# Plain down chunks of a decoder trunk streamed as two products of 256 columns, with one order of terms

## The chip, the cores and the metric

The kernel runs on one core of a Trainium2 chip. The time is the device time of one execution in microseconds (us), and the number that counts is the median of several runs. The kernel before takes 1089.61 us, median of 3 runs from 1089.52 to 1090.16.

## The reference

One decoder layer over 256 tokens with 2048 features, all in float32: a normalised input goes through one projection to q, k, v and gates, two groups of eight attention heads follow, their outputs are projected back and added; then a squared-ReLU MLP with 8192 hidden features, and a last norm.

```python
h = rms_norm(x, norm1_g[l])
proj = h @ w_in[l]                      # 2048 -> 6152
...
x = x + mixed @ w_out[l]                # 2048 -> 2048
h = rms_norm(x, norm2_g[l])
x = x + jnp.square(jax.nn.relu(h @ w_mlp_in[l])) @ w_mlp_out[l]   # 2048 -> 8192 -> 2048
return rms_norm(x, final_norm_g)
```

The change lies in the last matrix product, with `w_mlp_out`: the down projection.

## The kernel before, in words

**Products in parts.** Each float32 operand is split into an upper part, which TensorE takes exactly (`hi`), and the rest (`lo`). A product of x and w is then three: x_hi w_hi, x_lo w_hi and x_hi w_lo, added up in PSUM. One operand stands in the array (an LDWEIGHTS of 128 x 128 ahead of each product), the other is streamed past it. A row of the profile such as `acc<-whi,big_lo` names the streamed operand first and the standing one second.

**Chunks and steps.** The weights are read in chunks of 512 columns. A chunk of the MLP has 16 tiles of 128 rows (`kt`), two of them to a step. For each step SyncE loads weights (`raw`, one megabyte for two steps), ScalarE writes the upper part (`whi`, L253) and VectorE the lower (`wlo`, L254), some steps ahead of the products, into a ring of tiles that the products give back.

**The MLP** goes in four rounds of 2048 hidden features. The chunks come in these forms:

- Up chunks ("u"): the weights stand, the activations `aT_hi`, `aT_lo` are streamed, 256 wide (`turned_product`, L417). Their results are squared and split into `big_hi`, `big_lo`, and a mixed form of them into `mix_hi`, `mix_lo`.
- Mixed down chunks (set `seven`): a form with seven block products instead of eight, which takes sums of weights and of activations. Here the activations stand and the weights are streamed, 256 wide, in the order hi hi, hi lo, lo hi (`seven_products`, L461). Each unit of four row tiles has four sub-steps: near, first, odd, even.
- Plain down chunks: the activations `big_hi`, `big_lo` stand, 128 tokens at a time, the weights are streamed 512 wide (`product`, L401). There are two in each round, and in the last round three.

The list `steps` (L138 to L159) sets the order by hand. A round opens with its four up chunks, among which the first down chunk of the round before is mixed in. Then comes a plain chunk by itself (8 steps), and after it four units of: near, first, odd of the second down chunk, a plain step of the third, even, another plain step. The last round opens with chunk 0 by itself and closes with chunk 3, the kernel's last. That one (`last_chunk`, L862) first does all 16 row tiles for the first 128 tokens, 512 wide, then twice for the second 128 tokens, 256 wide each, so that the end of the work on the first block lies beside products. Its first three steps of split weights go to the tiles of `aT_hi`, `aT_lo`, which are free by then.

**Order of the terms.** For the plain down chunks `product` takes the three terms in an order that `ORDERS` gives for each round: standing part and streamed part are hi hi, lo hi, hi lo in rounds 0 and 3; lo hi, hi hi, hi lo in round 1; hi lo, hi hi, lo hi in round 2. The last chunk uses hi hi, lo hi, hi lo. The attention's chunks that use `product` (v and o) have this order too.

**Places of the tiles.** All tiles that TensorE reads start at chosen offsets within 64 elements (constants L43 to L45). The split weights of plain down chunks and of the mixed steps both start at 8 (`NEAR`); `big_hi` and `big_lo` start at 32 and 48.

Of the kernel before, what the change touches and what calls it, by code (L numbers as in the profile page):

```python
# [28 lines left out]
CW = 512  # L29
# [13 lines left out]
LINE, NEAR, HIGH, LOW, GATED = 64, 8, 24, 56, 48  # L43
MIX_HI, MIX_LO = 24, 32
BIG_HI, BIG_LO = 32, 48  # L45
ORDERS = ((0, 1, 2), (1, 0, 2), (2, 0, 1), (0, 1, 2))
TURNED = "qku"
WARM, WARM2 = 8, 3

# [27 lines left out]
def kernel(  # L77
# [44 lines left out]
    for g, (vc, qc, kc, half, kind) in enumerate(groups):  # L122
        for what, c0 in (("q", qc), ("v", vc), ("k", kc)):
            cols = CW + NH if (g == 0 and what == "v") else CW
# [39 lines left out]
    raws, splits, spent = {}, {}, set()  # L164
# [62 lines left out]
    def split(i, j0=0, n=2):  # L227
        if i >= len(steps):
            return
        if j0:  # L230
            return split_rows(i, j0, n)
        ci, s, sub = steps[i]
        if sub:
            return split_seven(i)
        if ci == len(chunks) - 1 and s < 3:
            hi, lo = (a[:, 4 * s:4 * s + 4, :].rearrange("p (k j) s -> p k (j s)", k=2) for a in (aT_hi, aT_lo))
        else:
            what, cols = chunks[ci][0], chunks[ci][5]
            high, low = (HIGH, LOW) if what in TURNED else (NEAR, NEAR) if cols == CW else (GATED, HIGH - NEAR)
            hi, lo = (a.rearrange("p (j c) -> p j c", j=2) for a in part_tiles(i, 2 * cols, high, low))  # L240
        splits[i] = (hi, lo)
        split_rows(i, j0, n)
# [142 lines left out]
    accs = {}  # L385

    def operands(what, key):
        if what == "o":
            return yT_hi, yT_lo, key[0] * NH
        if what == "d":  # L390
            return *squares(), 0
        return aT_hi, aT_lo, 0

    def product(acc, a, kt, t, w, j, cols, go, end, order=(0, 1, 2)):

        (ah, al, base), (hi, lo) = a, w
        xh, xl = (p[:, base + kt, t * P:(t + 1) * P] for p in (ah, al))
        terms = ((xh, hi), (xl, hi), (xh, lo))
        for n, k in enumerate(order):
            x, part = terms[k]  # L400
            nc.tensor.matmul(acc, x, part[:, j, cols], start=go and n == 0, stop=end and n == 2,  # L401
                             skip_group_check=True)

    def turned_product(ci, i, j, kt, kts):


        if kt == 0:
            accs[ci] = [psum.tile([P, CW], F32, name="acc", bufs=4) for _ in range(2)]
        hi, lo = splits[i]
        terms = ((hi, aT_hi), (hi, aT_lo), (lo, aT_hi))  # L410
        order = [(b, n) for b in range(4) for n in range(3)]
        if i == j == 0:
            order.sort(key=lambda bn: bn[1])
        for b, n in order:
            acc = accs[ci][b // 2][:, b % 2 * SEQ:(b % 2 + 1) * SEQ]
            w, a = terms[n]
            nc.tensor.matmul(acc, w[:, j, b * P:(b + 1) * P], a[:, kt, :],  # L417
                             start=kt == 0 and b % 2 == 0 and n == 0, stop=kt == kts - 1 and n == 2,
                             skip_group_check=True)

    def products(i, j):
        ci, s, sub = steps[i]
        what, key, _, _, _, cols, kts = chunks[ci]
        if sub:
            return seven_products(i, j)
        kt = 2 * s + j
        if what in TURNED:
            return turned_product(ci, i, j, kt, kts)
        a = operands(what, key)
        if cols > CW:  # L430
            return gated_products(ci, i, j, kt, kts, a)
        if kt == 0:
            accs[ci] = [psum.tile([P, CW], F32, name="acc", bufs=4) for _ in range(TB)]
        go, end = kt == 0, kt == kts - 1
        order = ORDERS[key[0]] if what == "d" else (0, 1, 2)
        for t in range(TB):
            product(accs[ci][t], a, kt, t, splits[i], j, slice(0, CW), go, end, order)

    def seven_products(i, j):

        ci, s, sub = steps[i]
        if ci not in accs:
            accs[ci] = [psum.tile([P, CW], F32, name=n) for n in ("sc", "sc", "tr", "tr")]
        one_, two_, three, four = accs[ci]
        half, k1, k2 = CW // 2, 2 * s + j, 2 * s + 2 + j
        lower, upper = slice(0, P), slice(P, SEQ)
        h, m = squares(), (mix_hi, mix_lo)
        todo = {
            "near": ((one_, 0, h, k2, lower), (one_, half, m, k2, lower)),
            "first": ((three, 0, h, k1, lower),),  # L450
            "odd": ((two_, half, m, k2, upper), (four, 0, m, k1, upper)),
            "even": ((three, half, m, k1, lower), (two_, 0, h, k2, upper)),
        }[sub]
        begin = j == 0 and s == 0
        hi, lo = splits[i]
        for n, (bank, c0, (ah, al), k, tokens) in enumerate(todo):
            acc = bank[:, c0:c0 + half]
            fresh = begin and (bank, sub) in ((one_, "near"), (three, "first"), (two_, "odd"), (four, "odd")) and (
                bank is not one_ or n == 0)
            for x, (a, w) in enumerate(((ah, hi), (ah, lo), (al, hi))):  # L460
                nc.tensor.matmul(acc, a[:, k, tokens], w[:, j, n * half:(n + 1) * half], start=fresh and x == 0,  # L461
                                 stop=s == KT // 2 - 2 and j == 1 and x == 2, skip_group_check=True)

    def gated_products(ci, i, j, kt, kts, a):

        if kt == 0:
            accs[ci] = [psum.tile([P, 512], F32, name=n, bufs=k) for n, k in (("acc", 4), ("acc", 4), ("sc", 2))]
        half = CW // 2
        for t in range(TB):
            for acc, c0, c1, go in ((accs[ci][0][:, t * half:(t + 1) * half], 0, half, t == 0),  # L470
                                    (accs[ci][1 + t][:, :half + NH], half, CW + NH, True)):
                product(acc, a, kt, t, splits[i], j, slice(c0, c1), go and kt == 0, kt == kts - 1)
# [261 lines left out]
    def squares():  # L734
        return rows_at(big_hi, BIG_HI), rows_at(big_lo, BIG_LO)
# [86 lines left out]
    def add_down(acc, t, cs, n):  # L822

        nc.vector.scalar_tensor_tensor(
            xs[:, t, cs], acc[:, :cs.stop - cs.start], rstd2sq[:, t:t + 1], xs[:, t, cs], op0=ALU.mult, op1=ALU.add
        )
        if n is not None:
            if cs.stop < D_MODEL:
                square_and_gain(t, cs, n)
            else:  # L830
                unused = two.tile([P, CW], F32, name="nat")
                unused, xc, total = unused[:, :cs.stop - cs.start], xs[:, t, cs], ssq3[:, t, n:n + 1]
                nc.vector.tensor_tensor_reduce(unused, xc, xc, 1.0, 0.0, ALU.mult, ALU.add, total)
# [4 lines left out]
    def sum_before(t, n):  # L838
        s = ssq3s[:, t:t + 1]
        nc.vector.tensor_reduce(s, ssq3[:, t, :n], axis=mybir.AxisListType.X, op=ALU.add)  # L840
        nc.vector.tensor_scalar(s, s, D_MODEL * EPS, None, op0=ALU.add)
# [20 lines left out]
    def last_chunk(done):  # L862

        ci = len(chunks) - 1
        what, key, _, _, _, _, kts = chunks[ci]
        i0 = len(steps) - kts // 2
        c0 = D_MODEL - CW
        for t, a, b, n in ((0, 0, CW, 3), (1, 0, CW // 2, 3), (1, CW // 2, CW, 4)):
            acc = psum.tile([P, CW], F32, name="acc", bufs=4)
            for kt in range(kts):  # L870
                if t == 0 and kt % 2 == 0:
                    split(done + 1 + kt // 2)
                product(acc[:, :b - a], operands(what, key), kt, t, splits[i0 + kt // 2], kt % 2, slice(a, b),
                        kt == 0, kt == kts - 1)
                if t == 0:
                    run_side(2 * i0 + kt)
            if b == CW:
                sum_before(t, n)
            add_down(acc, t, slice(c0 + a, c0 + b), n)
            if b == CW:  # L880
                finish(t, n, slice(c0 + a, c0 + b))


    def run_side(n):
        for f, a in side.get(n, []):
            f(*a)

    for ci, (what, key, *_rest) in enumerate(chunks[:-1]):
# [9 lines left out]
        elif what in "qk":  # L898
# [3 lines left out]
            if what == "k":  # L902
                kind = groups[key][4]
                for h in range(4):
                    n = e + 6 + 7 * (h // 2)
# [63 lines left out]
    for i in range(final):  # L969
# [30 lines left out]
        for j in range(2):  # L1000
            products(i, j)
            run_side(2 * i + j)
    last_chunk(done)


# [28 lines left out]
```

## Time and profile before

| | |
|---|---|
| median of the runs | 1089.61 us (1089.52 to 1090.16) |
| the profiled execution | 1087.94 us |
| its span, first to last instruction | 1086.2 us |
| granted TensorE clock, mean | 0.997 |
| TensorE: busy, products | 1073.9 us, 7877 |
| weight loads: busy, loads | 1007.0 us, 7877 |
| VectorE, ScalarE, GpSimd busy | 800.3, 604.4, 28.0 us |
| read from memory | 205.93 MB |

PE is the product side of TensorE and PEld its weight loads, which go on beside the products; DVE is VectorE, ACT ScalarE, POOL GpSimd, SP SyncE. The profile gives for each group of instructions a busy time and a mean duration, but products overlap in the array: the next starts before the one ahead has ended. The chain of waits follows the work that ended last back to the beginning, and shows unbroken stretches of one line with their start, their length and the number of instructions. The windows give the busy time of each engine between two times, with the number of instructions. The attention ends and the MLP begins at 393.6 us.

### The profile page before, as it was taken

The numbers are of one execution on the slowest core, as the hardware profiler recorded it, in microseconds if no ns is written. First come the engines' busy times: TensorE is split into PE (matmuls) and PEld (weight loads), VectorE is DVE, ScalarE is ACT, GpSimd is POOL, SyncE is SP. The second block draws the span as 40 slices with busy tenths as digits, with TensorE's granted clock in tenths as the row PEclk, the third lists the DMA queues.
The fourth block names the chain that finished last, engine by engine and source line by source line (L and its number), as shares of the span: only waits on it lengthen the run. The fifth ranks groups of instructions, "written<-read, shape, count | busy, mean of one in ns | idle before, by whom it ended". The sixth has DMA issues, their size and how long they took to land.

```text
span 1086.2 us, 18976 instructions
## 1 busy us (share of the span) xinstructions
PE 1073.9 (99%) x7877; PEld 1007.0 (93%) x7877; DVE 800.3 (74%) x1076; ACT 604.4 (56%) x821; POOL 28.0 (3%) x42
## 2 busy tenths in 40 slices
PE   8999999999999999999999999999999999999996
PEld 7999899998988899998999998899998999999886
DVE  6667756667577666568877788887778886778885
ACT  6555545545454555565546665556665545666561
POOL 0010200000001000000000000000000000000000
PEclk9999999999999999999999999999999999999998
DMA  9764564655545566655675655665656665656552
GB/s 322 237 228 161 157 199 149 194 165 181 199 155 185 164 184 210 193 190 192 203 215 193 203 197 171 208 203 174 204 204 210 187 195 187 195 195 232 193 195 78
DMA packets 105394, 209.26 MB, mean 193 GB/s; under 512 B 3971, under 2 KB 5084, under 8 KB 105180
## 3 DMA queue, kind: packets, MB, share of 16 engines
q1 hardware_dynamic: 104412, 206.59, 58.3%
q8 instruction: 61, 1.00, 0.4%
q0 software_dynamic: 304, 1.06, 0.3%
q10 hardware_dynamic: 592, 0.40, 0.2%
q14 instruction: 25, 0.20, 0.1%
HBM read 205.93 MB, written 2.11 MB: 192 GB/s over the span
## 4 chain that ended last, share of the span: by engine, by line
PE 99%; DMA 0%; DVE 0%; POOL 0%; ACTq 0%; DVEq 0%; issue 0%
PE acc L417 48%; PE acc L401 34%; PE sc L461 7%; PE tr L461 5%; PE tr L350 1%; PE sc L691 1%; PE sc L401 1%; PE sc L647 1%; PE tr L675 0%; DMA xs<-in_x_dram 0%; PE sc L643 0%; PE sc L693 0%; PE sc L637 0%; PE sc L641 0%; DVE xs L859 0%; PE sc L695 0%
## 5 line engine op out<-in xcount | busy, mean ns | idle before, releaser
L254 DVE TENSOR_TENSOR wlo<-raw,whi 128x1024 fp32r<-128x1024 f32 (+2 forms) x327 | 394.0, 1220 | 155.2 <-ACT whi L253 152.9
L253 ACT ACTIVATE whi<-raw 128x1024 fp32r<-128x1024 f32 (+2 forms) x328 | 339.3, 1050 | 223.5 <-PE acc L417 130.4
L417 PE MATMUL acc<-aT_hi,whi 128*128 128x256 f32 x1536 | 425.6, 277 | 0.0
L417 PE MATMUL acc<-aT_hi,wlo 128*128 128x256 f32 x1536 | 424.0, 276 | 0.0
L417 PE MATMUL acc<-aT_lo,whi 128*128 128x256 f32 x1536 | 423.8, 276 | 0.0
L417 PEld LDWEIGHTS acc<-aT_hi,whi 128*128 128x128 f32 x1536 | 288.2, 188 | 1.2 <-issue 0.9
L417 PEld LDWEIGHTS acc<-aT_lo,whi 128*128 128x128 f32 x1536 | 288.2, 188 | 0.3
L417 PEld LDWEIGHTS acc<-aT_hi,wlo 128*128 128x128 f32 x1536 | 288.1, 188 | 0.1
L401 PE MATMUL acc<-whi,big_lo 128*128 128x512 f32 (+1 forms) x414 | 160.8, 388 | 0.0
L401 PE MATMUL acc<-whi,big_hi 128*128 128x512 f32 (+1 forms) x414 | 160.3, 387 | 0.0
L401 PE MATMUL acc<-wlo,big_hi 128*128 128x512 f32 (+1 forms) x414 | 160.0, 386 | 0.0
L401 PEld LDWEIGHTS acc<-wlo,big_hi 128*128 128x128 f32 x414 | 77.8, 188 | 15.9
L401 PEld LDWEIGHTS acc<-whi,big_lo 128*128 128x128 f32 x414 | 77.7, 188 | 15.2
L401 PEld LDWEIGHTS acc<-whi,big_hi 128*128 128x128 f32 x414 | 77.7, 188 | 15.2
L219 ACT ACTIVATE whi<-both 128x1024 fp32r<-128x1024 f32 x56 | 59.7, 1067 | 52.6 <-DVE both L224 24.8
L220 DVE TENSOR_TENSOR wlo<-both,whi 128x1024 fp32r<-128x1024 f32 x56 | 68.3, 1220 | 7.5 <-ACT whi L219 6.5
L337 DVE TENSOR_TENSOR big_lo<-nat,big_hi 128x512 fp32r<-128x512 f32 x32 | 22.2, 693 | 43.7 <-ACT big_hi L336 43.7
L401 PE MATMUL acc<-whi,aT_hi 128*128 128x512 f32 (+1 forms) x144 | 51.7, 359 | 0.0
L401 PE MATMUL acc<-whi,aT_lo 128*128 128x512 f32 (+1 forms) x144 | 51.0, 354 | 0.0
L401 PE MATMUL acc<-wlo,aT_hi 128*128 128x512 f32 (+1 forms) x144 | 51.0, 354 | 0.0
L219 ACT ACTIVATE whi<-raw 128x1024 fp32r<-128x1024 f32 x28 | 29.6, 1058 | 11.8 <-PE acc L401 6.4
L336 ACT ACTIVATE mix_hi<-nat 128x512 fp32r<-128x512 f32 x32 | 18.5, 625 | 29.9 <-DVE nat L761 29.9
(212 smaller groups left out, 1351.2 us busy)
## 6 DMA issues: line engine op xcount, KB each, us to landing
raw<-in_w_mlp_in_dram SPq DMA_DIRECT2D x64, 1024.0 KB, 5.7
raw<-in_w_mlp_out_dram SPq DMA_DIRECT2D x64, 1024.0 KB, 5.1
raw<-in_w_in_dram SPq DMA_DIRECT2D x42, 1024.0 KB, 5.1
raw<-in_w_out_dram SPq DMA_DIRECT2D x16, 1024.0 KB, 5.0
raw<-in_w_in_dram SPq DMA_DIRECT2D x4, 1040.0 KB, 8.5
xs<-in_x_dram SPq DMA_DIRECT2D x3, 512.0 KB, 9.7
raw<-in_w_in_dram SPq DMA_DIRECT2D x2, 512.0 KB, 5.4
big_lo<-rel_d POOLq DMA_DIRECT2D x1, 1024.0 KB, 7.2
```

Of the source, the lines that this page charges most:

```text
L219: nc.scalar.activation(hi, src, AF.Copy)
L220: nc.vector.tensor_tensor(lo, src, hi.bitcast(F32), op=ALU.subtract)
L253: nc.scalar.activation(hi[:, :, c:c + step], t[:, :, c:c + step], AF.Copy)
L254: nc.vector.tensor_tensor(lo, t, hi.bitcast(F32), op=ALU.subtract)
L336: nc.scalar.activation(hi, src, AF.Copy)
L337: nc.vector.tensor_tensor(lo, src, hi.bitcast(F32), op=ALU.subtract)
L350: nc.tensor.transpose(p[:, j * SEQ + t * P:j * SEQ + (t + 1) * P], xs[:, t, c:c + P], ident)
L401: nc.tensor.matmul(acc, x, part[:, j, cols], start=go and n == 0, stop=end and n == 2, skip_group_check=True)
L417: nc.tensor.matmul(acc, w[:, j, b * P:(b + 1) * P], a[:, kt, :], start=kt == 0 and b % 2 == 0 and n == 0, stop=kt == kts - 1 and n == 2, s ...
L461: nc.tensor.matmul(acc, a[:, k, tokens], w[:, j, n * half:(n + 1) * half], start=fresh and x == 0, stop=s == KT // 2 - 2 and j == 1 and x ...
L647: nc.tensor.matmul(s[:, c0:c1], q[:, a, h, rows], k[:, b, h, keys], start=False, stop=n == 2, skip_group_check=True)
L691: nc.tensor.matmul(y[:, :SEQ], v[:, 0, dims], p[:, m, :SEQ], start=n == 0, stop=False, skip_group_check=True)
```

## The change

Three things are changed, all on TensorE.

- In the plain down chunks each product of 512 columns becomes two of 256, the left half with all its three terms first, then the right half. This holds for the first token block of the last chunk as well; its second block was in halves already.
- All plain down products take the terms in the order hi hi, hi lo, lo hi (standing, streamed). So the upper standing part is loaded twice in a row, then the lower part once. `ORDERS` goes.
- The flag that begins a sum in a PSUM bank stands on the first product of the left half alone.

```diff
-ORDERS = ((0, 1, 2), (1, 0, 2), (2, 0, 1), (0, 1, 2))
...
-    def product(acc, a, kt, t, w, j, cols, go, end, order=(0, 1, 2)):
+    def product(acc, a, kt, t, w, j, cols, go, end, narrow=False):
 
         (ah, al, base), (hi, lo) = a, w
         xh, xl = (p[:, base + kt, t * P:(t + 1) * P] for p in (ah, al))
-        terms = ((xh, hi), (xl, hi), (xh, lo))
-        for n, k in enumerate(order):
-            x, part = terms[k]
+        for n, (x, part) in enumerate(((xh, hi), (xh, lo), (xl, hi)) if narrow else ((xh, hi), (xl, hi), (xh, lo))):
             nc.tensor.matmul(acc, x, part[:, j, cols], start=go and n == 0, stop=end and n == 2,
                              skip_group_check=True)
...
-        order = ORDERS[key[0]] if what == "d" else (0, 1, 2)
+        parts = 2 if what == "d" else 1
         for t in range(TB):
-            product(accs[ci][t], a, kt, t, splits[i], j, slice(0, CW), go, end, order)
+            for c in range(0, CW, CW // parts):
+                cols = slice(c, c + CW // parts)
+                product(accs[ci][t][:, cols], a, kt, t, splits[i], j, cols, go and c == 0, end, parts > 1)
...
-        for t, a, b, n in ((0, 0, CW, 3), (1, 0, CW // 2, 3), (1, CW // 2, CW, 4)):
+        half = CW // 2
+        for t, a, b, n in ((0, 0, CW, 3), (1, 0, half, 3), (1, half, CW, 4)):
             acc = psum.tile([P, CW], F32, name="acc", bufs=4)
             for kt in range(kts):
                 if t == 0 and kt % 2 == 0:
                     split(done + 1 + kt // 2)
-                product(acc[:, :b - a], operands(what, key), kt, t, splits[i0 + kt // 2], kt % 2, slice(a, b),
-                        kt == 0, kt == kts - 1)
+                for c in range(a, b, half):
+                    product(acc[:, c - a:c - a + half], operands(what, key), kt, t, splits[i0 + kt // 2], kt % 2,
+                            slice(c, c + half), kt == 0 and c == a, kt == kts - 1, True)
```

TensorE's queue at the start of the first plain chunk, in round 0, before: `acc_5310` and `acc_5311` are the sums of the two token blocks, and a wait for DVE is the one for the lower half of the weights.

```order
L417 MATMUL acc_5059<-aT_hi_131,wlo_5151 128x256
L401 MATMUL acc_5310<-whi_5180,big_hi_146 128x512 [waits Activation_49]
L401 MATMUL acc_5310<-whi_5180,big_lo_145 128x512
L401 MATMUL acc_5310<-wlo_5181,big_hi_146 128x512 [waits DVE_49]
L401 MATMUL acc_5311<-whi_5180,big_hi_146 128x512 [waits PE_49]
```

The same place after; `product` has moved up by three lines, from L401 to L398.

```order
L414 MATMUL acc_5059<-aT_hi_131,wlo_5151 128x256
L398 MATMUL acc_5310<-whi_5180,big_hi_146 128x256 [waits Activation_49]
L398 MATMUL acc_5310<-wlo_5181,big_hi_146 128x256 [waits DVE_49]
L398 MATMUL acc_5310<-whi_5180,big_lo_145 128x256
L398 MATMUL acc_5310<-whi_5180,big_hi_146 128x256
L398 MATMUL acc_5310<-wlo_5181,big_hi_146 128x256
L398 MATMUL acc_5310<-whi_5180,big_lo_145 128x256
L398 MATMUL acc_5311<-whi_5180,big_hi_146 128x256 [waits PE_49]
```

Six products stand where three stood, and the one that waits for VectorE is the second instead of the third.

The end of that chunk and the first products of the mixed step behind it, before (`sc_5466` is a sum of the mixed chunk):

```order
L401 MATMUL acc_5311<-whi5_5366,big_hi_146 128x512
L401 MATMUL acc_5311<-whi5_5366,big_lo_145 128x512
L401 MATMUL acc_5311<-wlo5_5367,big_hi_146 128x512
L461 MATMUL sc_5466<-whi_5386,big_hi_146 128x256 [waits Activation_49]
L461 MATMUL sc_5466<-wlo_5387,big_hi_146 128x256 [waits DVE_49]
L461 MATMUL sc_5466<-whi_5386,big_lo_145 128x256
```

And after:

```order
L398 MATMUL acc_5311<-whi5_5402,big_hi_146 128x256
L398 MATMUL acc_5311<-wlo5_5403,big_hi_146 128x256
L398 MATMUL acc_5311<-whi5_5402,big_lo_145 128x256
L460 MATMUL sc_5562<-whi_5434,big_hi_146 128x256 [waits Activation_49]
L460 MATMUL sc_5562<-wlo_5435,big_hi_146 128x256 [waits DVE_49]
L460 MATMUL sc_5562<-whi_5434,big_lo_145 128x256
```

Ahead of the mixed step there is now a row of products of its own width, order and standing tiles. In all, TensorE has 816 products more, each with its load. On the other engines the same instructions stand in the same order.

## The prediction

> **What bounds the kernel now.** I read the page first, then the waits of TensorE, then the chain that ended last. From the page and from the waits:
>
> ```profile
> PE 99%; DMA 0%; DVE 0%; POOL 0%; ACTq 0%; DVEq 0%; issue 0%
> PE tr L350 <- DMA xs<-in_x_dram: 1.9, 1, 1.9
> PE sc L317 <- DVE relx L294: 1.2, 1, 1.2
> ```
>
> TensorE is 99% of the chain, and these two are its only waits (us in total, times, longest): 3.1 us, both at the start. So the time is the number of products times their pitch, the distance from one start to the next. The mean durations in the groups are no use for that: products overlap, and their ends are modelled. The pitch is read from the chain, where a row has start, length, line and count of an unbroken stretch:
>
> ```profile
> 297.27 8.19 PE acc L401 x36
> ...
> 481.68 22.25 PE acc L401 x96
> 503.93 1.41 PE sc L461 x12
> ...
> 507.39 2.78 PE acc L401 x12
> ...
> 556.31 1.36 PE sc L461 x12
> ...
> 563.79 19.04 PE acc L417 x168
> ...
> 651.51 22.25 PE acc L401 x96
> ...
> 821.23 22.25 PE acc L401 x96
> ...
> 991.23 22.25 PE acc L401 x96
> ...
> 1048.02 2.78 PE acc L401 x12
> ...
> 1052.18 24.82 PE acc L401 x156
> ```
>
> L417 is the up projection, all of it 256 wide: 19.04 / 168 = 113.3 ns a product. From 481 us on, L401 is the plain down chunks, 512 wide: 22.25 / 96 = 231.8 ns, the same to the hundredth in all four rounds. Two products of 256 at 113.3 cover the same columns in 226.7. So a plain down product takes 5.1 ns longer than its columns need. That is not the width as such: the 512-wide products of the first o chunk (the row at 297.27) take 8.19 / 36 = 227.5.
>
> The starts around the end of a plain chunk, from the timeline of TensorE:
>
> ```profile
> 503.31 0.39 PE L401 MATMUL acc<-whi,big_lo 128*128 128x512 f32 x1
> 503.54 0.39 PE L401 MATMUL acc<-wlo,big_hi 128*128 128x512 f32 x1
> 503.77 0.28 PE L461 MATMUL sc<-whi,big_hi 128*128 128x256 f32 x1
> ...
> 504.84 0.28 PE L461 MATMUL sc<-whi,mix_hi 128*128 128x256 f32 x1
> ...
> 505.18 0.28 PE L461 MATMUL tr<-fhi,big_hi 128*128 128x256 f32 x1
> ...
> 506.54 0.28 PE L461 MATMUL sc<-whi,mix_hi 128*128 128x256 f32 x1
> ```
>
> From 503.77 to 504.84 lie nine 256-wide products, 1.07 / 9 = 118.9 ns each. From 505.18 to 506.54 lie twelve, 1.36 / 12 = 113.3. The first nine carry on the slow manner of the 512-wide stream: about 5 ns more per product, whatever its width. Then the stream falls into step by itself and stays there. I read the 5 ns as a disturbance that comes once per product, from how its weight load falls against the streaming of the one before, and that a row of 256-wide products settles out of; what inside the array does it, the trace does not show.
>
> **The change part by part.**
>
> *Width, the main term.* Products that change: the four opening chunks have 4 x 96 = 384 in 4 x 22.25 = 89.00 us. The plain steps among the mixed ones are 32 pieces of 12, 384 products: 31 are rows of their own, the first and last quoted, 2.77 or 2.78 us each, and the 32nd opens the last row; 32 x 2.78 = 88.96. The first token block of the last chunk is 48, at 231.7 ns 11.12 (check: 24.82 - 60 x 0.2317 = 10.92 for that row's 96 narrow products, 113.8 each). Sum: 816 products, 189.08 us. After: 1632 products at 19.04 / 168 = 113.33 ns, 184.96. Gain 4.12 us. I take 113.3 because the new products are the mixed step's products in all that I can see: same order of terms, same tiles in the same places, same stationary big_hi and big_lo, same width; and those run at 113.3 once settled. Bounds: 118.9, the unsettled rows, would make 194.0, a loss of 5.0; below 113.3 no row goes by more than the rounding.
>
> *What follows a plain stretch.* With no 512-wide stream ahead, the mixed products start settled. From the windows, restricted to L461, behind plain steps and then inside the up projection:
>
> ```profile
> 503.77:507.22 3.45, 3.45 (x30) 1.00 0.02 7
> 510.00:511.38 1.38, 1.38 (x12) 1.00 0.40 154
> 514.16:517.58 3.42, 3.42 (x30) 1.00 0.60 229
> 556.14:559.54 3.40, 3.40 (x30) 1.00 0.75 255
> 562.26:563.62 1.36, 1.36 (x12) 1.00 1.08 372
> ```
>
> Per round the first of these comes once, 3.45 against 3.40. The piece of 12 behind a unit's first plain step comes four times, 1.38 against 1.36, and the piece of 30 behind its second plain step three times, 3.42 against 3.40. Together 0.05 + 7 x 0.02 = 0.19, times four rounds 0.76. Not every round need show all of it; I take 0.7, bounds 0 and 0.76.
>
> *Weight loads.* 816 more loads. What hides them, from the groups kept apart by shape and from the windows of all engines:
>
> ```profile
> L401 PEld LDWEIGHTS acc<-whi,big_lo 128*128 128x128 f32 x64 | 12.0, 188 | 2.4
> 481.52:503.77 22.25, 22.25 (x98) 18.03 (x97) 17.20 (x21) 12.86 (x17) 0.00 (x0) 1.00 0.54 189
> 507.22:517.58 10.36, 10.36 (x68) 9.31 (x67) 8.94 (x11) 5.85 (x6) 0.00 (x0) 1.00 0.62 203
> 563.79:582.80 19.01, 19.01 (x170) 19.01 (x170) 12.80 (x16) 11.46 (x15) 0.00 (x0) 1.00 0.53 162
> ```
>
> In the window at 563.79 there is a load for each 256-wide product, 170 in 19.01 us, and loads fill the whole of it, each record 188 ns long at a pitch of 113.3. So a load per 113.3 ns is sustained, and I cost the extra loads at nothing; the cover is the streaming of one product. The Trainium skill (TensorE: Matmul & The Clock Gate, LDWEIGHTS) puts a load at its columns over 1.2 GHz, an estimate of 107 ns for these 128. By that the cover shrinks to some 6 ns, but still holds, and the rows agree. If it failed, each product would take the pitch of a load instead, which is the first rival. That the upper part is now loaded twice in a row saves no load: in the mixed steps, which already do that, products and loads are equal in number.
>
> *Order of terms.* The product that reads the low weight half moves from third to second place, and in round 2 from first to second. Its wait for VectorE then comes 0.46 - 0.11 = 0.35 us earlier in a step. Cover: the waits above show no wait of TensorE for VectorE or ScalarE after the start, while ScalarE waits for TensorE to give tiles back:
>
> ```profile
> ACT whi L253 <- PE acc L401: 59.6, 42, 2.1
> ```
>
> The splitting is ahead and held back by the products. Cost 0; without that cover it would be at most 0.35 for each of 72 plain steps.
>
> *Faster TensorE, same other work.* VectorE has 17.20 us of work in a plain stretch of 22.25, and 8.94 in a mixed unit of 10.36 (the second number of instructions in a window is PEld's, then VectorE, ScalarE). The unit loses 24 x 5.1 ns, to 10.24; VectorE goes from 86% to 87%. DMA is at 0.54 to 0.62. No other engine's instructions change or move past a queue. The chain behind the last product is untouched.
>
> Sum: 4.1 + 0.7 = 4.8 us less. The profiled execution took 1087.94 (span 1086.2, 1.7 around it) and would take 1083.1; the median of the runs is 1089.61, 1.7 above the profiled one, so the forecast there is 1084.8.
>
> **The rivals.**
>
> *Unsettled, slower.* The plain products stay at the pitch after 503.77: the 5.1 ns is a price of each weight load against big_hi and big_lo tiles, and doubling the loads doubles it. Price: 816 x 5.1 = 4.2 us by the present excess, 5.0 by the nine products: 1093.8 to 1094.6. It decides from a pitch of 231.7 / 2 = 115.9 ns on. For it: nothing in the trace is a long run of 256-wide products with big_hi and big_lo alone until the last chunk. Against it: those 96, in the old order, ran at 113.8 with their start included, and L461 alternates big and mix tiles at 113.3.
>
> *Half settled.* The stream settles but is thrown out again at each change of step or token block, and stays near 114.5: 1632 x 1.2 ns = 2.0 of the gain lost, and some of the 0.7: about 1087.
>
> *Not the width at all.* Something else in those windows (traffic of DMA, ScalarE, VectorE) slows the streaming by 2%, and two halves take 231.7 together: no change, 1089.6. Against it: L461 runs at 113.3 in the same windows, with VectorE busier, and the pitch is the same in four rounds.
>
> *A fixed price per product.* 816 more products each cost a start, on top of the present pitch. From rows: 227.5 for the o chunk's 512 against 2 x 113.3 leaves no such price; I allow 1 ns, 0.8 us, 1090.4. The Trainium skill (TensorE: Matmul & The Clock Gate, Back-to-back issue gap) gives a warm product its columns over 2.4 GHz plus about 2.5 ns. By that rule splitting loses 816 x 2.5 ns, an estimate of 2.0 us, to 1091.6. These rows do not bear it out: 113.3 for 256 columns is not shortened per column by going to 512.
>
> **How the numbers follow.** Forecast 0.76, half settled 0.08, unsettled 0.08, not the width 0.05, fixed price 0.03. Time 1084.8. About 0.2%, 2.2 us, is what a measurement of this kernel can tell from no change, so "faster" ends at 1087.4. Faster: 0.76 and most of half settled, 0.82. Same: the rest of half settled, not the width and most of the fixed price, 0.09. Slower: unsettled and the remainder, 0.09. The forecast's own bounds: 1632 products 0.3 ns either way, 0.5 us, all of the second term lost, and 0.3 for the spread of the runs: 1084.0 to 1086.3. To hold 8 in 10 the upper end goes on through half settled, to 1087.2; the lower end is 1083.8.
>
> **What would show it.** In the chain of the changed kernel, the four opening stretches become about 192 products in 21.76 us (or merge with their neighbours at that pitch), the pieces of 24 take 2.72, and the mixed stretches behind them 3.40 and 1.36. TensorE's waits stay at the two of the start. The forecast is wrong if the plain products stand at 115 ns or more, if a wait of TensorE for VectorE appears in the down rounds, or if the pitch falls as told and the span does not.

## The result, and the profile after

In the runs made for the comparison the changed kernel takes 1082.32 us (median of 5, 1082.24 to 1083.53), beside 1090.15 us for the kernel before (median of 5, 1089.52 to 1090.49). The ratio of the runs is 0.9946, with a 95% interval from 0.9935 to 0.9957. It is not the ratio of these two medians, which is 0.9928: the five runs of the kernel before were slower than most of its later ones, and 0.9946 is what the mean of the changed kernel's five, 1082.76, gives over the mean of all 30 fast runs of the kernel before on record, 1088.6 us. On the 1089.61 us from which the forecast started the ratio gives 1083.7 us, which is 5.9 us less, between 4.7 and 7.1: faster by more than the 0.2% that the prediction took for what can be told, and by less than 1%. The profiled execution took 1082.24 us with a span of 1080.4, against 1087.94 and 1086.2.

TensorE waits at the same two places as before, at the start (us in total, times, longest):

```profile
PE sc L316 <- DVE relx L293: 1.2, 1, 1.2
PE tr L349 <- DMA xs<-in_x_dram: 1.2, 1, 1.2
```

The chain that ended last, with start, length, line and count; L398 is `product`, L414 the up products, L460 the mixed ones:

```profile
296.99 8.19 PE acc L398 x36
...
397.05 84.34 PE acc L414 x744
481.39 21.76 PE acc L398 x192
503.15 1.36 PE sc L460 x12
...
506.55 2.72 PE acc L398 x24
...
650.03 21.76 PE acc L398 x192
...
818.67 21.76 PE acc L398 x192
...
987.31 21.76 PE acc L398 x192
...
1047.15 24.49 PE acc L398 x216
```

The opening stretch of 22.25 us has become 21.76: 192 products at 113.3 ns, in all four rounds. The pieces among the mixed steps take 2.72 instead of 2.78, and the last row, now of one width, 24.49 / 216 = 113.4 ns. The first mixed products after a plain stretch no longer start at 118.9; twelve of them take 1.36 us at once. The windows of L460 behind plain steps show the same for the other joints of round 0, 3.39, 1.36 and 3.40 against 3.45, 1.38 and 3.42 before:

```profile
503.00:506.39 3.39, 3.39 (x30) 1.00 0.08 30
509.11:510.47 1.36, 1.36 (x12) 1.00 0.67 259
513.19:516.59 3.40, 3.40 (x30) 1.00 0.72 276
```

In the windows of all engines the loads now fill the whole of a plain stretch and of a mixed unit, as they did in the up projection (after the time: PE, PEld, DVE, ACT, POOL, clock, DMA):

```profile
481.23:503.00 21.77, 21.77 (x195) 21.77 (x194) 16.92 (x21) 12.87 (x17) 0.00 (x0) 1.00 0.55 190
506.39:516.59 10.20, 10.20 (x93) 10.20 (x91) 8.97 (x10) 5.85 (x6) 0.00 (x0) 1.00 0.62 207
```

Where the time came from: the plain products take 4 x 21.76 + 32 x 2.72 + 96 x 0.1133 = 184.96 us, 4.12 less. From the start of the long row of 744 up products (397.34 before, 397.05 after) to the end of the last product (1077.00 before; after, 1047.15 + 24.49 = 1071.64) it is 679.66 and 674.59, 5.07 less. The other 0.95 of that is the products behind plain stretches. By the starts in the trace the mixed steps of the four rounds' plain parts take 19.04 us each, where they took 19.24, 19.13, 19.42 and 19.23: 0.85 in all. The last 0.1 lies in the up products behind the third chunk and in the last block. What is left, 0.7 of the span's 5.8, lies at its two ends, in code that is as before: 0.3 ahead of the MLP, where the first wait for `in_x` was 1.9 and is 1.2, and 0.4 behind the last product. No run shows that the change brings these.

### The profile page after: what moved, and what is told of

It is laid out like the page before. It is cut to its first block, busy times and chain, and to the rows that moved or that the text cites. A ratio compares the mean times of both kernels' runs of the same rounds, so it can differ in the third digit from the quotient of the medians.

```text
span 1080.4 us, 20584 instructions
## 1 busy us (share of the span) xinstructions
PE 1069.3 (99%) x8693; PEld 1037.8 (96%) x8693; DVE 800.2 (74%) x1076; ACT 604.4 (56%) x821; POOL 27.9 (3%) x42
## 4 chain that ended last, share of the span: by engine, by line
PE 99%; DMA 0%; DVE 0%; POOL 0%; ACTq 0%; DVEq 0%; issue 0%
PE acc L414 48%; PE acc L398 34%; PE sc L460 7%; PE tr L460 5%; PE tr L349 1%; PE sc L690 1%; PE sc L398 1%; PE sc L646 1%; PE tr L674 0%; DMA xs<-in_x_dram 0%; PE sc L642 0%; PE sc L692 0%; PE sc L636 0%; PE sc L640 0%; DVE xs L858 0%; PE sc L694 0%
## 5 line engine op out<-in xcount | busy, mean ns | idle before, releaser
L414 PE MATMUL acc<-aT_hi,whi 128*128 128x256 f32 x1536 | 425.4, 277 | 0.0
L414 PE MATMUL acc<-aT_hi,wlo 128*128 128x256 f32 x1536 | 423.8, 276 | 0.0
L414 PE MATMUL acc<-aT_lo,whi 128*128 128x256 f32 x1536 | 423.7, 276 | 0.0
L414 PEld LDWEIGHTS acc<-aT_hi,whi 128*128 128x128 f32 x1536 | 288.2, 188 | 1.1 <-issue 0.9
L414 PEld LDWEIGHTS acc<-aT_lo,whi 128*128 128x128 f32 x1536 | 288.2, 188 | 0.1
L414 PEld LDWEIGHTS acc<-aT_hi,wlo 128*128 128x128 f32 x1536 | 288.1, 188 | 0.1
L398 PE MATMUL acc<-whi,big_hi 128*128 128x256 f32 (+1 forms) x680 | 202.8, 298 | 0.0
L398 PE MATMUL acc<-wlo,big_hi 128*128 128x256 f32 (+1 forms) x680 | 202.3, 297 | 0.0
L398 PE MATMUL acc<-whi,big_lo 128*128 128x256 f32 (+1 forms) x680 | 202.2, 297 | 0.0
L398 PEld LDWEIGHTS acc<-wlo,big_hi 128*128 128x128 f32 x680 | 127.6, 188 | 5.1
L398 PEld LDWEIGHTS acc<-whi,big_lo 128*128 128x128 f32 x680 | 127.7, 188 | 4.7
L398 PEld LDWEIGHTS acc<-whi,big_hi 128*128 128x128 f32 x680 | 127.6, 188 | 4.7
L398 PE MATMUL acc<-whi,aT_hi 128*128 128x512 f32 (+1 forms) x144 | 51.7, 359 | 0.0
L398 PE MATMUL acc<-whi,aT_lo 128*128 128x512 f32 (+1 forms) x144 | 51.0, 354 | 0.0
L398 PE MATMUL acc<-wlo,aT_hi 128*128 128x512 f32 (+1 forms) x144 | 51.0, 354 | 0.0
```

## The experiments

All times are beside runs of the kernel before on the same chip. Its medians in these jobs lay between 1087.4 and 1088.2 us, lower than in the first comparison; the stretches of the chain repeat to a few hundredths of a microsecond, so the verdicts are read there. Where one run is named, the time is that of a single execution.

**The places, counted from the memory.** Ahead of the prediction `big_hi` and `big_lo` are said to start at 32 and 48 within 64 elements, and the expectations below count in the same way. These are offsets inside the two tiles, and the tiles do not begin at a multiple of 64. One after another lie 8 elements (`ahead`), `aT_hi` and `aT_lo` of 4096 each, `big_lo` of 4096 + 48 and `big_hi` of 4096 + 32. In the program built from the kernel `big_lo` begins at byte 139296 of a partition and `big_hi` at byte 155872; in elements of four bytes that is 8 and 56 beyond a multiple of 64. So the lower part stands at 8 + 48 = 56, and the upper at 56 + 32 = 88, which is 24. By their addresses `mix_hi` and `mix_lo` lie at 24 and 56. The weights that stand in the up chunks are at 24 and 56 too, and what is streamed past all of these is at 8. Every row that the prediction read at 113.3 ns has these places.

Below, places are those in the memory. Offsets of 16 and 0 put both parts at 8, the place of the streamed tile. That is where the standing tiles of the attention's o and v chunks are as well.

**Halves in the old orders.** The changed kernel with `ORDERS` back in `product`:

```diff
+        order = ORDERS[key[0]] if what == "d" else (0, 1, 2)
...
-                product(accs[ci][t][:, cols], a, kt, t, splits[i], j, cols, go and c == 0, end, parts > 1)
+                product(accs[ci][t][:, cols], a, kt, t, splits[i], j, cols, go and c == 0, end, order)
```

> The plain down products are halves of 256, but keep the old orders of terms by round (hi hi, lo hi, hi lo in rounds 0 and 3; lo hi, hi hi, hi lo in round 1; hi lo, hi hi, lo hi in round 2). Theory (the width does it: a stream of 256 wide products falls into step in any order): the four opening stretches take 21.76 us for 192 products each, 113.3 ns a product, and the time is that of the changed kernel, about 1082 to 1084 us. Rival (the order does it, two loads of the upper part in a row): at least rounds 1 and 2, where the upper part is not loaded right behind itself within a triple, stay at 115.5 to 119 ns a product, 22.2 to 22.8 us a stretch, and 1 us or more of the gain is lost.

The four opening stretches in the chain:

```profile
481.66 21.76 PE acc L401 x192
...
650.30 21.76 PE acc L401 x192
...
818.94 21.76 PE acc L401 x192
...
987.58 21.76 PE acc L401 x192
```

The expectation had the rounds wrong: it is in rounds 0 and 3 that the upper part is not loaded twice in a row within a triple (in rounds 1 and 2 it is). Across the triples of one row tile it is so in every order. All four stretches are at 21.76. The time is 1083.23 us, ratio 0.995 (0.9938 to 0.9962), which is that of the changed kernel. These orders bring nothing at this width.

**The new order, 512 wide.**

```diff
-ORDERS = ((0, 1, 2), (1, 0, 2), (2, 0, 1), (0, 1, 2))
+ORDERS = ((0, 2, 1),) * 4
```

The last chunk gets the same order.

> The plain down products stay 512 wide, but take the new order hi hi, hi lo, lo hi in all rounds and in the last chunk. Theory (width): 231 to 232 ns a product, 22.2 to 22.3 us for each opening stretch of 96, and a time within 0.5 us of the kernel before. Rival (order): 226.7 to 228 ns, 21.8 to 21.9 us, and 3 to 4 us less than before.

```profile
481.47 22.26 PE acc L401 x96
...
1052.59 24.82 PE acc L401 x156
```

Both rows are those of before, within 0.01 us, and the ratio is 1.0007 (0.9998 to 1.0016). So the whole gain is that of the halves.

**512 wide, the streamed tiles moved.**

```diff
+            if what == "d":
+                high = low = (8, 24, 40, 56)[chunks[ci][1][0]]
```

> 512 wide as before, but the split weights that the plain chunks stream start at 8, 24, 40 and 56 elements within 64 in rounds 0, 1, 2 and 3. Theory (the 512 wide stream cannot fall into step whatever the place): all four opening stretches 22.2 to 22.3 us. Rival (the disturbance is a clash of the places of the streamed and the standing tile, and the width only lets a stream slide away from it): the stretches differ by round, between 21.8 and 22.8 us, with round 0 at 22.25.

```profile
483.37 22.25 PE acc L403 x96
...
653.19 22.19 PE acc L403 x96
...
822.99 22.40 PE acc L403 x96
...
993.33 22.39 PE acc L403 x96
```

The offsets 8, 24, 40 and 56 are places in the memory here. The stretches differ by round, as the rival has it: by 22.40 - 22.19 = 0.21 us, 2.2 ns a product. But none of the four places brings the 512 wide stream near 21.76, as the theory has it. The next run decides. (The time of the one run is 1090.98 us; its first plain stretch starts 1.7 us later than before, ahead of anything that was changed.)

**512 wide, the standing tiles moved**, from 24 and 56 to 8 and 8 (offsets 16 and 0):

```diff
-        return rows_at(big_hi, BIG_HI), rows_at(big_lo, BIG_LO)
+        return rows_at(big_hi, BIG_HI - 16), rows_at(big_lo, 0)
```

> 512 wide as before, but the standing activations start at 16 and 0 within 64 instead of 32 and 48, which are the places of the o chunks' standing tiles, whose first stretch ran at 227.5 ns a product. Theory (width alone): the opening stretches stay at 22.2 to 22.3 us for 96. Rival (place): they come to 21.8 to 21.9 us, 227 to 228 ns a product. The mixed steps may change as well, up or down by a few us in all, since their places change too.

```profile
481.50 21.79 PE acc L401 x96
...
1052.25 25.15 PE acc L401 x156
```

21.79 / 96 = 227.0 ns: 512 wide products go at full pitch with their standing tiles there. The theory of the width alone falls. And the last row has slowed: its 60 wide products at 227.0 ns leave 25.15 - 13.62 = 11.53 us for the 96 narrow ones, 120.1 ns each against 113.8 before. What helps the one width harms the other. The mixed steps, 256 wide, slow down as well, by the starts in the trace from 134.1 to 137.3 us in all, and the kernel is back at 1088.49 us (one run).

**The change with those places.** The same line, in the changed kernel:

> The changed kernel with the standing activations of the down projection at 16 and 0 instead of 32 and 48. Theory (pair of place and width): the plain products stay at 119.9 ns as the last chunk did in the run of the kernel before with these places, the opening stretches take 23.0 us instead of 21.76, the mixed steps about 4 us more in all, and the time is 1095 to 1098 us: with these places the change would be a loss. Rival (256 wide settles by itself when enough of it stands in a row, the last chunk was too short or too special): 21.8 to 22.2 us a stretch, and 1083 to 1087 us.

```profile
481.33 23.04 PE acc L398 x192
```

23.04 / 192 = 120.0 ns, the same in all four rounds, and 1097.62 us in the one run, 9.7 us above the 1087.95 of the kernel before in that job. Against the changed kernel it is 15 us more: 1728 products x 6.7 ns make 11.5 us, and the mixed steps take 137.4 us in place of 133.3. The same halving is a gain with the standing parts at 24 and 56 and a loss with both at 8.

**Halves in the attention's chunks as well.** In the changed kernel all ungated chunks are halved. The expectation has the standing tiles at 16 and 0 for o and at 8 and 8 for v; in the memory both are at 8 and 8:

```diff
-        parts = 2 if what == "d" else 1
+        parts = 2
```

> The changed kernel, with the o chunks and the three ungated v chunks as halves of 256 in the new order as well. Their standing tiles lie at 16 and 0 (o) and at 8 and 8 (v). Theory as corrected by the run with the standing tiles moved (the pair of place and width decides, and at 16 and 0 a 256 wide stream does not settle, 119.9 ns): the o stretches get longer, about 239.8 ns for the former 512 against 227.5 to 230, some 4 us more over the 384 former products; for v no run tells, 226.7 to 240. Rival (a 256 wide stream settles anywhere, the 119.9 came from the last chunk alone): o at 226.7 ns, about 1 us less than the changed kernel.

The first o stretch, which was 8.19 us for 36 products of 512, and the first v stretch:

```profile
106.27 5.75 PE acc L398 x48
...
300.55 8.64 PE acc L398 x72
```

8.64 / 72 = 120.0 ns, and 5.75 / 48 = 119.8: the same places, and nearly the same pitch, in other chunks with other tiles. Both lose, 8.1 us in all: 1090.40 us in the one run against 1082.3.

**o in halves, with its standing tiles at 24 and 56** (offsets 32 and 48).

```diff
-        parts = 2 if what == "d" else 1
+        parts = 2 if what in "do" else 1
...
-    yT_hi, yT_lo = rows_at(big_hi, BIG_HI - 16), rows_at(big_lo, 0)
+    yT_hi, yT_lo = rows_at(big_hi, BIG_HI), rows_at(big_lo, BIG_LO)
```

> The changed kernel, with the o chunks as halves of 256 too, and their standing activations moved from 16 and 0 to 32 and 48, the places of the down projection's. Theory (pair of place and width): o at 113.3 ns, 226.7 for a former 512 instead of 227.5 to 230, 0.5 to 1.0 us less than the changed kernel. Rival (something else in the attention's tail, as its mixed stream with transposes and small products, keeps the o products up): no gain.

```profile
297.32 8.16 PE acc L398 x72
...
361.94 10.90 PE acc L398 x96
```

The move undoes the loss: 8.16 / 72 = 113.3 ns. But nothing is won, since 8.19 for 36 whole products was at full pitch already; the second row stands against 10.91 us for 48 before. The expected 0.5 to 1.0 us did not come. The ratio of 0.995 (0.9936 to 0.9963) is the changed kernel's. No experiment gave a version that beats the change.

**Other widths.** To see how much cover a weight load has, the plain columns are cut in another way in each round of the changed kernel: 128 wide in round 0; halves under one term before the next in round 1; 384 and 128 in round 2; halves as in the change in round 3.

```diff
+            cuts = (((0, 128), (128, 256), (256, 384), (384, 512)), ((0, 256), (256, 512)),
+                    ((0, 384), (384, 512)), ((0, 256), (256, 512)))[key[0]]
```

> The changed kernel, with another cut of the plain steps' 512 columns in each round: round 0 four products of 128, round 1 two of 256 but both under one term before the next term (upper part loaded four times in a row), round 2 384 and 128, round 3 two of 256 as in the change. It measures how much cover a weight load has left. Theory (a load goes on beside one product, and 113.3 ns is just enough for it): with 128 the load sets the pitch, at 107 to 113 ns a product instead of 56.7, so the opening stretch of 384 products in round 0 takes 41 to 44 us; round 1 and round 3 take 21.76 us; in round 2 a pair of 384 and 128 takes 226.7 only if the short one's load is hidden, and more likely 170 + 107 to 113, 26.5 to 27.5 us for the stretch. Rival (loads are never the limit here, and the 5 ns was a clash of places): 128 wide products go at 57 to 62 ns, 21.8 to 23.8 us, and all four stretches are about as long.

```profile
482.69 42.83 PE acc L398 x384
...
693.69 21.76 PE acc L406 x192
...
862.33 27.26 PE acc L398 x192
...
1042.55 21.76 PE acc L398 x192
```

And some of the loads of round 0, from the timeline:

```profile
489.90 0.19 PEld L398 LDWEIGHTS acc<-wlo,big_hi 128*128 128x128 f32 x1
490.01 0.19 PEld L398 LDWEIGHTS acc<-whi,big_lo 128*128 128x128 f32 x1
490.12 0.19 PEld L398 LDWEIGHTS acc<-whi,big_hi 128*128 128x128 f32 x1
490.23 0.19 PEld L398 LDWEIGHTS acc<-wlo,big_hi 128*128 128x128 f32 x1
```

128 wide: 42.83 / 384 = 111.5 ns, not 57. Over the whole stretch the loads start 111 or 112 ns apart without exception, while the starts of the products scatter between 108 and 115: it is the loads that keep the pace, one in 111.5 ns. The 113.3 of a 256 wide product covers that with 1.8 ns to spare. In round 2 three products of 384 come in a row and then three of 128. The six take 27.26 / 32 = 852 ns; at 0.443 ns a column the long ones make 3 x 170 of it, which leaves 114 for each short one, about a load. How often the same part is loaded in a row (round 1) plays no part.

**The same cuts, both standing parts at 8.** Both edits together:

> The kernel that cuts the plain columns by round (128 in round 0; two of 256 under one term in round 1; 384 and 128 in round 2; two of 256 in round 3), now with the standing activations at 16 and 0. It asks where the 119.9 ns come from. Theory A (a load itself takes longer from these places): 128 wide products, which the load bounds, go at 119 to 121 ns instead of 111.5, 45.7 to 46.5 us for the opening stretch in round 0 instead of 42.8, and then a 256 wide stream of 113.3 is simply below the load, and a 512 wide one of 226.9 hides it. Theory B (the load is as fast, and it clashes with a 256 wide stream beside it): 111 to 112 ns, 42.6 to 43.0 us. Both: 23.0 us in rounds 1 and 3.

```profile
481.50 42.83 PE acc L398 x384
...
693.67 23.04 PE acc L406 x192
```

42.83 again: from these places a load is as fast as from the others. So the 120.0 ns come neither from the load by itself (111.5) nor from the streaming by itself (113.5, half of the 227.0 at these places). What is left is that the two hold each other up when they go on at once; that is argued from the two bounds and not shown. The two kernels with these cuts take 1137.38 and 1147.40 us (one run each), the 128 wide round above all.

**One part moved**, each in the changed kernel: upper at 24 and lower at 8 (offsets 32 and 0); upper at 8 and lower at 56 (16 and 48); and a third run with both offsets at 32. That one was meant to put both parts at one place, but in the memory it has the upper part at 24 and the lower at 40. The first edit:

```diff
-        return rows_at(big_hi, BIG_HI), rows_at(big_lo, BIG_LO)
+        return rows_at(big_hi, BIG_HI), rows_at(big_lo, 0)
```

> The changed kernel with only the lower standing part moved, upper at 32 and lower at 0. A place that acts load by load gives one slow product in three, (2 x 113.3 + 119.9) / 3 = 115.5 ns, 22.2 us for each opening stretch. If the places of the two parts act together, as a relation between neighbouring loads, it is 113.3 or 119.9 for all, 21.76 or 23.0 us.

> The changed kernel with only the upper standing part moved, upper at 16 and lower at 48, the counterpart of the run with only the lower part moved (117.7 ns a product, all three alike). If each moved load adds its part to a stream that shares it out, the upper part, with two loads of three, gives more than 117.7, 118 to 119.9 ns, 22.7 to 23.0 us for each opening stretch. If what counts is that both parts lie in one half of the 64, 32 to 63, it is again about 117.7, 22.6 us. If the upper part's place does not matter, 113.3, 21.76 us.

> The changed kernel with both standing parts at the same place, 32. If the place that counts is that against the streamed tile (at 8), 32 and 48 being both good ones, it stays at 113.3 ns, 21.76 us for each opening stretch. If what counts is the difference between neighbouring loads, it changes, to between 115 and 119.9 ns, 22.1 to 23.0 us.

The opening stretch of each in turn:

```profile
481.39 22.61 PE acc L398 x192
```

```profile
483.20 22.61 PE acc L398 x192
```

```profile
481.27 22.70 PE acc L398 x192
```

117.8, 117.8 and 118.2 ns, and 1093.91, 1093.74 and 1095.04 us (one run each). With the upper part moved, the starts in the timeline are uneven:

```profile
490.10 0.28 PE L398 MATMUL acc<-whi,big_hi 128*128 128x256 f32 x1
490.22 0.28 PE L398 MATMUL acc<-wlo,big_hi 128*128 128x256 f32 x1
490.34 0.28 PE L398 MATMUL acc<-whi,big_lo 128*128 128x256 f32 x1
490.45 0.28 PE L398 MATMUL acc<-whi,big_hi 128*128 128x256 f32 x1
```

0.12, 0.12 and 0.11. Over the stretch, from each start to the next, the two products of the moved part take 119.3 and 120.7 ns, that of the lower part 113.3. With the lower part moved to 8 all three are nearly alike, 117.7, 118.3 and 117.3, though the upper part stands where it is in the good pair. With the lower part at 40 they take 119.0, 119.5 and 116.2: it is the unmoved upper part that has slowed most. So the place of a part against the streamed tile does not set the pitch of its products alone; that of its neighbour counts. The third run says nothing of two parts at one place; the runs with both at 8 do.

| upper and lower part, streamed at 8 | 256 wide | 512 wide |
|---|---|---|
| 24 and 56 | 113.3 ns | 231.8 ns |
| 8 and 8 | 120.0 | 227.0 |
| 24 and 8 | 117.8 | |
| 8 and 56 | 117.8 | |
| 24 and 40 | 118.2 | |

A rule that gives the pitch from the places does not follow from these runs. 24 and 56 is the one good set for 256 that they show, and the mixed form and the up chunks, both at 113.3, have it too.

## Why the prediction was right, and where its reading was not

**The main term** was right to the hundredth: 113.33 ns for 1632 products and 4.12 us. What carried it was the argument that the new products are the mixed step's products in tiles, places, terms and width. The runs show that the width was needed at these places, that the places were needed at this width, and that the order was not. Tiles and terms by themselves were not varied.

**The second term**, 0.7 with a bound of 0.76, came out at 0.85 in the mixed steps, and with the 0.1 in the up products and the last block at 0.95. Its size was right in part by luck: the bound is four times what round 0 shows, but the rounds gave 0.20, 0.09, 0.38 and 0.19. Rounds 1 and 2 had other orders of terms, and there the products behind wide ones had lost other amounts. With 4.12 the 0.95 makes the 5.07 between the two marks, and the forecast of 4.8 was low by 0.3. The 1083.7 us that the ratio gives lies at the lower end of the stated 1083.8 to 1087.2, 0.1 beyond it. What is left between 5.07 and 5.9 lies within the interval of the ratio; in the profile it is the two ends of the span, for which the prediction had no term.

**Weight loads at no cost** was right, but closer than the prediction had it. It took a load's need from the up projection as 113.3 or less; the 128 wide round measures 111.5, so the cover is 1.8 ns. By the Trainium skill (TensorE: Matmul & The Clock Gate, LDWEIGHTS) the load would take an estimate of 107 ns, which leaves 6; the measurement decides.

**Order of terms at no cost**: right, by the two runs on the order. The wait for VectorE that moved forward never showed among TensorE's waits, and VectorE's load of 8.97 us in a mixed unit of 10.20 left TensorE unhindered.

**The reading of the 5 ns** was wrong, in the step that says a disturbance comes once per product and "a row of 256-wide products settles out of" it. A row of 256 wide products does not settle as such: with both standing parts at 8 it stays at 120.0 for whole stretches, in the plain chunks and in o, and at 119.8 in v. A row of 512 wide ones does get rid of it there, at 227.0. It is the pair of width and places that counts. All the settled rows that the prediction had were 256 wide and also stood at 24 and 56; it put down to the width what the two did together. It had the row that points there, the o chunk's 227.5 at 512, and used it only to say that the width as such is not slow. The forecast held because the new products keep those places.

**The rivals.** *Unsettled, slower* did not happen, but its mechanism exists: with other places the halves stand at 120.0 ns, above its deciding point of 115.9, and the time is above that of before. *Not the width at all* in the form of traffic from other engines falls: the moved tiles change the pitch with the same traffic. *A fixed price per product* falls with 1632 products at 113.33, the same per column as the fastest 512. By the formula of the Trainium skill (TensorE: Matmul & The Clock Gate, Back-to-back issue gap), which it gives for a product by itself, the halves would have lost an estimated 2.0 us, at estimates of 109 ns for 256 columns and 216 for 512. The rows, with 113.3 and 227.0 at best, do not follow it. *Half settled* was not seen at 24 and 56; pitches between the two ends did show with one part moved.

**What stays open** is what in the array or in the memory makes the pitch depend on the places, and whether 64 elements is the period that counts. The same page of the Trainium skill (TensorE: Matmul & The Clock Gate, Step-by-step: what each phase is for) says that streaming and loading read through two independent ports, so that a load takes no bandwidth from the running product. No run here looks at the ports; but with both parts at 8 a 256 wide product takes 120.0 ns, where the load by itself needs 111.5 and the stream 113.5, so in these rows the two are not free of each other.

## What to carry to other kernels

The pitch of products is read from unbroken stretches in the chain, length by count, and compared per column between stages of the same kernel; 2% of difference at the same clock was worth 5 us here. If two stages differ, list what differs between them (width, places of streamed and standing tiles, order) and make the slow one like the fast one in all of it, not in the one that seems to explain it: the same halving gained 5 us here and lost 8 elsewhere in the same kernel. Count the place of a tile from its address, not from an offset within it: two offsets that look different were one place here, and two that look alike were two. And in this kernel a product should not be cut below 256 columns, since a load wants 111.5 ns: 128 wide, a plain stretch took 42.83 us in place of 21.76.

## What the runs showed of the hardware beside this

- The place of the standing tiles within 64 elements, with the streamed tile at 8, changes the pitch of float32 products with nothing else changed: 113.3 and 120.0 ns at 256 wide (6%), 227.0 and 231.8 at 512 (2%).
- The best set for one width is not the best for the other: 24 and 56 for 256, both at 8 for 512, among those tried.
- A load of 128 x 128 in this format bounds the pitch at 111.5 ns, with the standing parts at 24 and 56 as with both at 8.
- After the stretch of 512 wide products at 24 and 56 that opens round 0, nine 256 wide ones run at 118.9 ns before they are at 113.3. In round 2, where the wide products ahead have another order of terms, the starts in the trace show three.
